# Sample keys turned on VectorE in 32x32 blocks and scored on sixteen 32x32 tiles of TensorE, with the value pages moved to the heads

## The chip, the cores and the metric

The kernel runs on one core of one Trainium2 chip. The metric is device time in microseconds, median of the runs shown. Engines are named as in the profile: PE is TensorE, PEld its weight loads, DVE is VectorE, ACT is ScalarE, POOL is GpSimd, SP issues the DMAs of this kernel.

## The reference

One inference step of a four-layer trunk (short convolution, gated recurrence, differential attention, short convolution) for a prompt of 1024 tokens and a sample group of 8 sequences with 4 new tokens each. The change is in the attention layer's sample group. Its past lies in pages of 128 tokens, found through a page table: 16 pages a sequence, 128 x 1024 float32 (512 KB) each for keys and for values.

```python
def diff_attn_sample(q, k_new, v_new, cache_k, cache_v, page_table, lam):
    bsz, t = q.shape[:2]
    k_past = cache_k[page_table].reshape(bsz, -1, 2 * N_HEADS, HEAD_DIM)
    v_past = cache_v[page_table].reshape(bsz, -1, N_HEADS, V_HEAD_DIM)
    n_past = k_past.shape[1]
    s_past = jnp.einsum('bqhd,bkhd->bhqk', q, k_past).astype(jnp.float32)
    s_new = jnp.einsum('bqhd,bkhd->bhqk', q, k_new).astype(jnp.float32)
    causal = jnp.tril(jnp.ones((t, t), dtype=bool))
    s_new = jnp.where(causal, s_new, -jnp.inf)
    p = jax.nn.softmax(jnp.concatenate([s_past, s_new], axis=-1), axis=-1)
    w = diff_combine(p, lam).astype(v_new.dtype)
    return (jnp.einsum('bhqk,bkhd->bqhd', w[..., :n_past], v_past)
            + jnp.einsum('bhqk,bkhd->bqhd', w[..., n_past:], v_new))
```

There are 16 half heads of 64 features and 8 heads whose values have 128. `diff_combine` subtracts `lam` times the second half head's probabilities from the first's.

## The kernel before, in words

The attention layer has three stages of prompt work. `qkv` makes the q, k and v projections, 512 columns (`n` from 0 to 5) and one 128-token tile (`t`) at a time: 24 matmuls of 128x512 a tile (`qk`, L798), 48 tiles in all. `zpath` makes the gate path (`zz`). `heads` runs prompt attention, head by head and 128 queries at a time: scores `S` (L914), exponentials `P`, transposes `wtp` and the product with the values `pv`.

The sample group is a generator, `sample`, whose steps are mixed into these three by `merge`: each main step adds a share of the sample's estimated cost to a debt, and sample steps run until the debt is paid. The shares are 0.08 and 0.18 in `qkv`, 0.06 in `zpath`, and the rest goes beside the heads. The written order is then arranged by a scheduler, which keeps each engine's dependences.

For each sequence and each pair of pages, `keys` loads two key pages (`kp`, SP, L1083), turns each with eight 128x128 TensorE transposes (`skt`, L1135), copies the result out of PSUM on VectorE and ScalarE in turn (`sk`, L1139), and multiplies the block-diagonal queries `qbd` with it on four column tiles of the array, 128 rows by 32 columns each (`sps`, L1116). `softmax` then makes one exponential over 2080 columns (L1150). `values`, one sequence behind, turns the probabilities (`spt`, L1160), loads value pages (`vp`) and multiplies on four column tiles again (`sacc`, L1175). Pages share four buffers.

A float32 matmul leaves two PE records in the trace: 512 `sps` matmuls of the pages and 64 of the new tokens are 1152 records, 512 `sacc` matmuls 1024.

`page` reads the page number from the table into a register of SP and issues the load from there; a load waits for its buffer to come free, with every later DMA of SP behind it.

Of the kernel before, what the change touches and what calls it, by code (L numbers as in the profile page):

```python
# [35 lines left out]
SAMPLE_COST = NB * (32 * 430 + 8 * 890 + 620 + 4 * 430 + 16 * 400 + 300 + 300.0)  # L36
# [8 lines left out]
class Trunk:  # L45
# [24 lines left out]
    # eight PSUM banks for the whole kernel; each phase deals its kinds of tiles out over the groups of banks  # L70
# [5 lines left out]
    def bank(self, kind, name):  # L76
        tag = next(self.deals[kind])
        return self.psum.tile([128, 512], F32, tag=tag, bufs=self.BANKS[tag], name=name)
# [32 lines left out]
    # keep `inst` behind `first` on their common engine  # L111
# [186 lines left out]
    # features 512 h to 512 h + 511 of one tile, token-major, and their statistics  # L298
# [35 lines left out]
    # the last LayerNorm, with its gain and bias along the rows  # L334
# [34 lines left out]
    # weights of the four products of feature block 0; all at once where the first block goes chunk by chunk  # L369
# [155 lines left out]
    def lru_layer(self, l, u, y, filler):  # L525
# [81 lines left out]
        for s, (kind, i) in enumerate(seq):  # L607
# [4 lines left out]
            elif kind == "xx":  # L612
                # chunks 0 and 1 of both blocks go before chunk 2, which is the last to be there
# [73 lines left out]
    def attn_consts(self, cp):  # L687
# [25 lines left out]
        self.qts = cp.tile([128, KB, S], F32, name="qts")  # L713
        self.kts = cp.tile([128, KB, S], F32, name="kts")
        self.pnew = cp.tile([128, 6, S], F32, name="pnew")
        self.late, self.k_done, self.v_done = [], False, False
# [4 lines left out]
    def qkv(self, u):  # L721
# [42 lines left out]
        def sample_rows(n):  # L764
# [6 lines left out]
            if kind == "q":  # L771
                nc.vector.tensor_scalar(rt[:S], rt[:S], -0.125, None, ALU.mult)
# [745 lines left out]
```

## Time and profile before

| | |
|---|---|
| median of 3 runs | 2516.6 us |
| lowest and highest | 2513.08 and 2520.77 us |
| profiled execution, span from first to last instruction | 2513.0 us (the page gives no other time of this execution) |
| PE, DVE, ACT, POOL busy | 2432.0, 1216.9, 897.1, 195.7 us |
| DMA | 364.14 MB, 145 GB/s on the mean |

The span is the time from the first to the last instruction of one execution on the chip. Busy time is the union of an engine's instructions, so work that overlaps on one engine counts once. A wait is told where the engine sat idle before an instruction, and is put down to what released it.

### The profile page before, as it was taken

What the parts mean: (1) busy time and instruction counts of PE and PEld (TensorE: products, weight loads), DVE (VectorE), ACT (ScalarE), POOL (GpSimd) and SP (SyncE); (2) the same over time, 40 slices, a digit from 0 to 9 for tenths busy, and PEclk for the clock granted to TensorE, in tenths of its full rate; (3) what the DMA queues carried; (4) which work ended last, traced back from release to release, by engine and by line L of the source; (5) the groups of instructions that cost most, each with busy time, mean ns of one, the idle gap of its engine ahead of it and who ended that gap; (6) DMA issues with size and microseconds to landing.
All of it is one profiled execution on the core that took longest, in us unless ns stands there. A gap on an engine that the chain in (4) does not pass through costs nothing.

```text
span 2513.0 us, 41867 instructions
## 1 busy us (share of the span) xinstructions
PE 2432.0 (97%) x16270; PEld 2110.8 (84%) x16270; DVE 1216.9 (48%) x2640; ACT 897.1 (36%) x1837; POOL 195.7 (8%) x329
## 2 busy tenths in 40 slices
PE   7999999999999999999999988989999999999997
PEld 5999999997888897777778966666667999999997
DVE  5323232467466546343323257777775453332355
ACT  4212221246454424122222256667663342222210
POOL 0000000001001000000000023232210000000000
PEclk9999999999999999999999999999999999999999
DMA  9223222433434525254578568888876321111132
GB/s 326 77 84 96 80 77 84 128 96 112 145 123 126 159 66 173 72 161 156 190 268 267 154 192 254 261 253 271 265 268 213 94 73 44 50 43 51 43 117 84
DMA packets 276715, 364.14 MB, mean 145 GB/s; under 512 B 15085, under 2 KB 192622, under 8 KB 276518
## 3 DMA queue, kind: packets, MB, share of 16 engines
q1 hardware_dynamic: 276518, 361.48, 46.3%
q8 instruction: 128, 2.10, 0.4%
q14 instruction: 69, 0.57, 0.1%
HBM read 313.94 MB, written 47.48 MB: 144 GB/s over the span
## 4 chain that ended last, share of the span: by engine, by line
PE 86%; DMA 10%; DVE 1%; ACT 1%; issue 1%; SPq 0%; POOL 0%; DVEq 0%; ACTq 0%; POOLq 0%
PE in L123 30%; PE op L123 15%; PE qk L798 10%; PE xb L123 4%; PE z L123 4%; DMA kp<-cache_k 4%; PE skt L1135 4%; PE zz L123 3%; PE ada L191 2%; PE S L914 2%; DMA tok<-kd 2%; PE sps L1116 2%; PE sacc L1175 2%; PE g L628 2%; PE pv L1009 2%; DMA vp<-cache_v 1%
## 5 line engine op out<-in xcount | busy, mean ns | idle before, releaser
L123 PEld LDWEIGHTS in<-ua,wi 128*128 128x128 f32 x4392 | 707.7, 188 | 22.6 <-issue 14.3
L123 PE MATMUL in<-ua,wi 128*128 128x384 f32 (+1 forms) x4392 | 722.4, 324 | 1.5 <-ACT wi L107 0.8
L798 PE MATMUL qk<-wq,ua 128*128 128x512 f32 x1152 | 288.6, 401 | 0.5 <-ACT qkr L802 0.5
L798 PEld LDWEIGHTS qk<-wq,ua 128*128 128x128 f32 x1152 | 210.6, 188 | 60.7 <-issue 10.8
L1135 PE MATMUL skt<-ident,kp 128*128 128x128 f32 x1024 | 143.2, 275 | 19.5 <-DMA kp<-cache_k 16.1
L1135 PEld LDWEIGHTS skt<-ident,kp 128*128 128x128 f32 x1024 | 115.3, 141 | 47.2 <-issue 12.7
L914 PE MATMUL S<-ks,qhl 128*128 128x512 f32 (+2 forms) x384 | 126.6, 416 | 8.0 <-ACT P L968 6.8
L968 ACT ACTIVATE P<-S,rr 128x512 f32<-128x512 f32 (+2 forms) x192 | 111.0, 584 | 26.7 <-DVE rr L959 14.9
L1139 DVE COPY sk<-skt 128x512 f32<-128x512 f32 x128 | 86.9, 686 | 67.9 <-PE skt L1135 47.8
L955 DVE TENSOR_REDUCE rr<-S 128x1 f32<-128x512 f32 (+2 forms) x192 | 104.2, 550 | 22.7 <-PE S L914 22.2
L283 DVE SCALAR_TENSOR_TENSOR r<-op,gate,xr 128x384 f32<-128x384 f32 (+1 forms) x96 | 54.2, 569 | 118.5 <-PE op L123 81.1
L431 DVE TENSOR_TENSOR sz<-in,sz 128x384 f32<-128x384 f32 (+1 forms) x48 | 25.2, 524 | 176.3 <-PE in L123 176.2
L1139 ACT COPY sk<-skt 128x512 f32<-128x512 f32 x128 | 75.1, 591 | 78.0 <-PE skt L1135 47.2
L123 PEld LDWEIGHTS z<-ub,wrz 128*128 128x128 f32 x576 | 92.6, 188 | 11.7 <-issue 10.1
L123 PE MATMUL zz<-ua,wz 128*128 128x384 f32 (+1 forms) x576 | 102.3, 329 | 0.0
L123 PEld LDWEIGHTS zz<-ua,wz 128*128 128x128 f32 x576 | 92.4, 188 | 7.1 <-issue 7.0
L123 PE MATMUL z<-ub,wrz 128*128 128x384 f32 (+1 forms) x576 | 98.2, 326 | 0.0
L123 PEld LDWEIGHTS xb<-ub,wrx 128*128 128x128 f32 x504 | 81.2, 188 | 12.7 <-issue 9.2
L123 PE MATMUL xb<-ub,wrx 128*128 128x384 f32 (+1 forms) x504 | 88.0, 328 | 0.0
L191 PE MATMUL ada<-wada,ct 128*32 128x512 f32 x384 | 82.9, 624 | 5.2 <-DMA wada<-w_ada 4.1
L1175 PE MATMUL sacc<-vp,pt 128*32 128x256 f32 x1024 | 73.7, 390 | 14.3 <-DMA vp<-cache_v 11.6
L914 PEld LDWEIGHTS S<-ks,qhl 128*128 128x128 f32 x384 | 67.9, 199 | 22.2 <-ACT P L968 10.1
(416 smaller groups left out, 3778.1 us busy)
## 6 DMA issues: line engine op xcount, KB each, us to landing
kp<-cache_k SPq DMA_DIRECT2D x128, 512.0 KB, 4.9
vp<-cache_v SPq DMA_DIRECT2D x128, 512.0 KB, 4.5
wada<-w_ada SPq DMA_DIRECT2D x96, 512.0 KB, 4.7
xa<-xat SPq DMA_DIRECT2D x64, 192.0 KB, 2.8
xr<-xa SPq DMA_DIRECT2D x64, 192.0 KB, 2.6
wi_2r<-a_w_in SPq DMA_DIRECT2D x16, 512.0 KB, 4.1
wi_0r<-a_w_in SPq DMA_DIRECT2D x16, 512.0 KB, 4.5
wi_3r<-a_w_in SPq DMA_DIRECT2D x16, 512.0 KB, 4.2
```

Of the source, the lines that this page charges most:

```text
L123: nc.tensor.matmul(ps[:, :n], wt[:, wp, k], self.ucols(units[k], up, c), start=i == 0, stop=i == 3 * KB - 1)
L191: nc.tensor.matmul(ps[c : c + 32, :], self.ct[:, k], wts[k // 2][:, k % 2], start=k < 4, stop=k >= 4, tile_position=(0, c),)
L283: nc.vector.scalar_tensor_tensor(r[:, :npr], ps[:, :npr], gate[:, d, 0:1], xt[:, :npr], ALU.mult, ALU.add)
L628: nc.tensor.matmul(ps[:, :n], wt[:, wp, q, k, m * 128 : (m + 1) * 128], self.ucols(y[2 * i + k], up, c), start=j == 0, stop=j == 5,)
L798: nc.tensor.matmul(ps, u[k][:, c0 : c0 + 128], wq[n, k // 2][:, wp, k % 2], start=i == 0, stop=i == 3 * KB - 1)
L914: nc.tensor.matmul(st[:, o : o + w], qs[h, g][:, part, s, 128 * qj : 128 * qj + 128], ks[h][:, s, l0 : l0 + w], start=part == 0, stop=part ...
L955: chain(nc.vector.tensor_reduce(rr[:, c : c + 1], t[:, :w], axis=AX.X, op=ALU.min))
L968: nc.scalar.activation(p[:, o : o + w], x["S"][s][i][:, :w], AF.Exp, scale=-1.0, bias=rr[:, 6 + s : 7 + s], accum_out=rr[:, c : c + 1])
L1009: nc.tensor.matmul(x["pv"], x["w"][kb // 4][:, j : j + 128], V[h][:, kb], start=kb == 0, stop=kb == qb)
L1135: nc.tensor.transpose(tp[:, 128 * g : 128 * g + 128], pg[j][:, 128 * h : 128 * h + 128], ident)
L1139: e(kt[:, :, 128 * j : 128 * j + 128], tp.rearrange("p (g t) -> p g t", g=4))
L1175: nc.tensor.matmul(acc[32 * g : 32 * g + 32, :], pts[0][:, 128 * (p % 4) + 32 * g : 128 * (p % 4) + 32 * g + 32], v[:, 256 * g : 256 * g + ...
```

## The change

It rewrites the sample group as two generators. `sample_keys` is mixed into `qkv` (share 0.78 of its cost) and `zpath` (0.24), and whatever is left of it runs out before the heads. `sample_values` is mixed into the heads.

In `sample_keys` a sequence is two halves of 8 pages. Each page is turned by one VectorE instruction, `nc.vector.transpose` on 32x32 blocks, into `kt` (one buffer, 8 pages); page buffers are three. A half is then scored by 128 matmuls of 32 rows, 32 columns and 256 moving columns, one for each of 16 positions of a 4x4 grid of tiles and each `k` of 8, into `psw`, one tile of four PSUM banks with one buffer. One ScalarE copy of 1024 columns takes it out, and the softmax of a sequence follows after its second half, once the new keys are known (`k_done`, set at the first tile of `n` = 3). The probabilities go to DRAM, 1 MB a sequence (`psd`), and `sample_values` reads them back, turns them, and gathers all 16 pages and the new rows in one accumulation. The sample rows of q and k are summed by a matmul with `sel` (`qss`) and turned by VectorE too.

```diff
-SAMPLE_COST = NB * (32 * 430 + 8 * 890 + 620 + 4 * 430 + 16 * 400 + 300 + 300.0)
+KEY_COST = NB * (16 * 300 + 2 * 4000 + 900.0)
+VALUE_COST = NB * (4 * 430 + 16 * 400 + 300 + 300.0)
...
         def sample_rows(n):
             kind, m = "qkv"[n // 2], n % 2
-            ps = acc.pop(n)
-            rt = self.pq.tile([128, 512], F32, tag="rt", bufs=4, name=f"qsr{n}")
-            nc.scalar.copy(rt[:S], ps[0:S])
-            for g in range(1, 4):
-                nc.vector.tensor_tensor(rt[:S], rt[:S], ps[S * g : S * g + S], ALU.add)
-            if kind == "q":
-                nc.vector.tensor_scalar(rt[:S], rt[:S], -0.125, None, ALU.mult)
+            pr = self.pq.tile([128, 512], F32, tag="rt", bufs=3, name=f"qsp{n}")
+            nc.scalar.copy(pr, acc.pop(n))
+            ps = self.tp(f"qss{n}")
+            nc.tensor.matmul(ps, self.sel, pr, start=True, stop=True)
+            rt = self.pq.tile([128, 512], F32, tag="rt", bufs=3, name=f"qsr{n}")
+            nc.scalar.mul(rt, ps, -0.125 if kind == "q" else 1.0)
             if kind == "v":
                 nc.sync.dma_start(
                     a["v_sample"][0, :, :, 4 * m : 4 * m + 4, :].rearrange("b t s f -> (b t) (s f)"), rt[:S]
                 )
                 nc.sync.dma_start(self.vsd[:, 512 * m : 512 * m + 512], rt[:S])
                 return
-            rope(rt, S, 8)
+            rope(rt, 128, 8)
             if kind == "k":
                 nc.sync.dma_start(
                     a["k_sample"][0, :, :, 8 * m : 8 * m + 8, :].rearrange("b t s f -> (b t) (s f)"), rt[:S]
                 )
-            ps = self.tp(f"qst{n}")
-            for j in range(4):
-                nc.tensor.transpose(ps[:, S * j : S * j + S], rt[:S, 128 * j : 128 * j + 128], self.ident[:S, :S])
-            dst = self.kts if kind == "k" else self.qts
-            self.k_done = n == 3
-            nc.vector.tensor_copy(dst[:, 4 * m : 4 * m + 4], ps[:, : 4 * S].rearrange("p (j t) -> p j t", j=4))
+            dst = self.qsb if kind == "q" else self.ksb
+            nc.vector.transpose(dst[:, 16 * m : 16 * m + 16].rearrange("p f t -> p (f t)"), rt)
+            self.q_done, self.k_done = self.q_done or n == 1, n == 3
...
-                if n == 0 and t == 1:
+                if n == 0 and t in (1, 2):
                     for e in range(2):
-                        fetch(0, 2 * e, "s")
-                        fetch(0, 2 * e + 1, "s")
-                        sample_half(0, e)
-                if t == (1 if n == 0 else 0):
+                        fetch(t - 1, 2 * e, "s")
+                        fetch(t - 1, 2 * e + 1, "s")
+                        sample_half(t - 1, e)
+                    sample_rows(t - 1)
+                if n > 1 and t == 0:
                     sample_rows(n)
-                if n < 5 and d in (2, 5):
+                if 0 < n < 5 and d in (2, 5):
                     sample_half(n + 1, d // 3)
                 yield 5120
...
+    def sample_keys(self):
+        nc = self.nc
+        ck, kp = self.pool("smpk", reuse_waits="tile", side="right")
+        self.sp_ = kp
+        self.cpb.__exit__(None, None, None)
+        cw, wp = self.pool("psw", space=PSUM, reuse_waits="tile")
+        self.qsb = kp.tile([128, 32, S], F32, name="qsb")
+        self.ksb = kp.tile([128, 32, S], F32, name="ksb")
+        qb = kp.tile([128, 4, 4, 2, 32], F32, name="qbd")
+        nc.gpsimd.memset(qb, 0.0)
+        half = NPG // 2
+        yield 0
+        while not self.q_done:
+            yield None
+        for b in range(NB):
+            qv = self.qsb.rearrange("p (g x h) t -> p g x h t", x=4, h=2)
+            for x in range(4):
+                nc.gpsimd.tensor_copy(qb[:, :, x, :, 4 * x : 4 * x + 4], qv[:, :, x, :, NQ * b : NQ * b + NQ])
+            qf = qb.rearrange("p g x h c -> p (g x h) c")
+            sc = kp.tile([128, NPG * 128 + S], F32, tag="S", bufs=1, name=f"sc{b}")
+            m = kp.tile([128, 8], F32, tag="smx", bufs=2, name=f"smx{b}")
+            for e in range(2):
+                kt = kp.tile([128, 32, half, 32], F32, tag="kt", bufs=1, name=f"kt{b}_{e}")
+                for j in range(half):
+                    pg = self.page("cache_k", b * NPG + half * e + j, f"kp{b}_{e}_{j}", 3)
+                    nc.vector.transpose(kt[:, :, j], pg.rearrange("p (f t) -> p f t", t=32))
+                    yield 300
+                ps = wp.tile([128, 4, 512], F32, tag="W", bufs=1, name=f"sps{b}_{e}")
+                for k in range(8):
+                    for g in range(4):
+                        for r in range(4):
+                            rows = slice(32 * r, 32 * r + 32)
+                            nc.tensor.matmul(
+                                ps[32 * g : 32 * g + 32, r, : 32 * half], qf[rows, 8 * g + k],
+                                kt[rows, 8 * g + k].rearrange("p j t -> p (j t)"), start=k == 0, stop=k == 7,
+                                tile_position=(32 * r, 32 * g))
+                o = sc[:, 128 * half * e : 128 * half * (e + 1)]
+                nc.scalar.copy(
+                    o.rearrange("p (j r t) -> p r j t", j=half, r=4),
+                    ps[:, :, : 32 * half].rearrange("p r (j t) -> p r j t", j=half))
+                nc.vector.tensor_reduce(m[:, e : e + 1], o, axis=AX.X, op=ALU.min)
+                yield 4000
+            while not self.k_done:
+                yield None
+            ps = self.tps(f"spn{b}")
+            for k in range(8):
                 for g in range(4):
                     nc.tensor.matmul(
+                        ps[32 * g : 32 * g + 32, :S], qf[0:32, 8 * g + k], self.ksb[0:32, 8 * g + k],
+                        start=k == 0, stop=k == 7, tile_position=(0, 32 * g))
+            o = sc[:, NPG * 128 :]
+            nc.vector.tensor_tensor(o, ps[:, :S], self.smask[:, b], ALU.add)
+            nc.vector.tensor_reduce(m[:, 2:3], o, axis=AX.X, op=ALU.min)
+            nc.vector.tensor_reduce(m[:, 3:4], m[:, 0:3], axis=AX.X, op=ALU.min)
+            nc.scalar.activation(sc, sc, AF.Exp, scale=-1.0, bias=m[:, 3:4], accum_out=m[:, 4:5])
+            nc.vector.reciprocal(m[:, 5:6], m[:, 4:5])
+            nc.vector.tensor_tensor(self.coef[:, b : b + 1], m[:, 5:6], self.srow, ALU.mult)
+            nc.sync.dma_start(self.psd[b], sc)
+            yield 900
+        cw.__exit__(None, None, None)
+        ck.__exit__(None, None, None)
+        self.cpb, self.psb = self.pool("psb2", space=PSUM, reuse_waits="tile")
+        self.keys_done = True
...
+    def sample_values(self, y):
+        nc = self.nc
+        ident = self.ident
+        cv, sp_ = self.pool("smpv", reuse_waits="tile", side="right")
+        self.sp_ = sp_
+        vs = sp_.tile([128, D], F32, name="vs")
+        nc.sync.dma_start(vs[:S], self.vsd)
+        def load(b):
+            sc = sp_.tile([128, NPG * 128 + S], F32, tag="S", bufs=2, name=f"sp{b}")
+            nc.sync.dma_start(sc, self.psd[b])
+            return sc
+        nxt = load(0)
+        yield 0
+        for b in range(NB):
+            sc, m = nxt, self.coef[:, b : b + 1]
+            if b + 1 < NB:
+                nxt = load(b + 1)
+            acc = self.tps(f"sacc{b}")[:, :256]
+            def apply(pt, v, k, first):
                 for g in range(4):
                     nc.tensor.matmul(
+                        acc[32 * g : 32 * g + 32, :], pt[:k, 32 * g : 32 * g + 32], v[:k, 256 * g : 256 * g + 256],
+                        start=first, stop=k == S, tile_position=(0, 32 * g))
+            for p0 in range(0, NPG + 4, 4):
+                tp = self.tps(f"spt{b}_{p0}")
+                n = 4 if p0 < NPG else 1
+                w = 128 if p0 < NPG else S
+                for j in range(n):
+                    c = 128 * (p0 + j)
+                    nc.tensor.transpose(tp[:w, 128 * j : 128 * j + 128], sc[:, c : c + w], ident)
+                pt = sp_.tile([128, 512], F32, tag="pt", bufs=2, name=f"pt{b}_{p0}")
+                nc.vector.tensor_copy(pt[:w, : 128 * n], tp[:w, : 128 * n])
+                yield 430
+                if p0 == NPG:
+                    apply(pt, vs, S, False)
+                    continue
+                for j in range(4):
+                    v = self.page("cache_v", b * NPG + p0 + j, f"vp{b}_{p0 + j}", 4)
+                    apply(pt[:, 128 * j : 128 * j + 128], v, 128, p0 + j == 0)
+                    yield 400
+            os_ = sp_.tile([128, 256], F32, tag="os", bufs=2, name=f"os{b}")
+            nc.vector.tensor_scalar(os_, acc, m, None, ALU.mult)
+            self.gather_o(b, os_)
+            yield 300
...
+        cq, self.pq = self.pool("pq", reuse_waits="tile")
+        self.deal(tp="U", tps="U", mm="R")
+        keys = self.sample_keys()
+        next(keys)
+        g = self.qkv(u)
+        for _ in range(3):
+            next(g)
+        merge(g, 45 * 5120.0, keys, self.shares[0] * KEY_COST)
+        cq.__exit__(None, None, None)
+        merge(self.zpath(u), 8 * 10.2 * NT, keys, self.shares[1] * KEY_COST)
+        rest(keys)
...
+        merge(main(), tot, values, VALUE_COST * self.ahead)
+        rest(values)
...
-            self.n_pg, self.n_kt = 4, 2
-            self.shares, self.ahead = (0.08, 0.18, 0.06), 1.2
+            self.shares, self.ahead = (0.78, 0.24), 1.1
```

Three places show what this does to the order of instructions. The first is PE in the projections, before, where the first key pages are turned: rows of `skt` (output, from identity and page `kp`) stand between those of `qk` (projection) and `qkf` (turned projection).

```order
L798 MATMUL qk_0_9759<-wq_3_9581,ua_82 128x512 x3
L1135 MATMUL skt_0_0_0_9854<-ident,kp_0_0_9829 128x128 x4
L1135 MATMUL skt_0_0_1_9860<-ident,kp_0_1_9841 128x128 x4
L1135 MATMUL skt_0_1_0_9867<-ident,kp_0_0_9829 128x128
L811 MATMUL qkf_5_9660<-ident,qkr_5_9652 128x128 x4
L1135 MATMUL skt_0_1_0_9867<-ident,kp_0_0_9829 128x128 x3
L798 MATMUL qk_1_9878<-wq_0_9379,ua_75 128x512 x3
```

PE in the projections, after the change, around the second half of one sequence and the first of the next (`kt_1` and `kt_0`).

```order
L804 MATMUL qk_5_12287<-wq_3_10451,ua_85 128x512 x3
L755 MATMUL qs_12096<-wq_2r,us 32x512 x2
L755 MATMUL qs_12096<-wq_3r,us 32x512 x2
L1129 MATMUL sps_1_11076<-kt_1_10971,qbd 32x256 x128
L1144 MATMUL spn_11725<-ksb,qbd 32x32 x32
L1129 MATMUL sps_0_11358<-kt_0_11253,qbd 32x256 x128
L817 MATMUL qkf_1_11849<-ident,qkr_1_11841 128x128 x4
L804 MATMUL qk_6_12477<-wq_0_10249,ua_78 128x512 x3
```

No `skt` is left; the scores stand in groups of 128, and here two groups follow each other with only the 32 small `spn` matmuls of the new tokens between them.

The second place is VectorE at the same point, with the semaphores that each instruction waits for: `kt` is written from the pages `kp`, one row a page.

```order
L1122 STREAM_TRANSPOSE kt_1_10971<-kp_1_7_11063 128x32x32 [waits DMAHW0_49]
L1122 STREAM_TRANSPOSE kt_0_11253<-kp_0_0_11254 128x32x32 [waits DMAHW1_49,DVE_49,PE_49]
L1122 STREAM_TRANSPOSE kt_0_11253<-kp_0_1_11267 128x32x32 [waits DMAHW2_49]
L1122 STREAM_TRANSPOSE kt_0_11253<-kp_0_2_11280 128x32x32 [waits DMAHW3_49]
L1137 TENSOR_REDUCE smx_10734<-sc_10733 128x1 [waits Activation_49]
L1122 STREAM_TRANSPOSE kt_0_11253<-kp_0_3_11293 128x32x32 [waits DMAHW4_49]
L1150 TENSOR_REDUCE smx_10734<-smx_10734 128x1 [waits DVE_49]
```

The first page of a half waits for PE, that is for the scores of the half before, and each page for its own load; the reductions of the softmax stand between them.

The third place is PE in the heads. Before, 16 transposes of one pair of key pages stand between the prompt's `wtp` and `pv`.

```order
L999 MATMUL wtp_6_512_15882<-ident,P_6_0_15592 128x128 x3
L1235 MATMUL sot_False<-ident,os_14232 128x128 x2
L1135 MATMUL skt_0_0_0_15378<-ident,kp_0_0_15353 128x128 x4
L1135 MATMUL skt_0_0_1_15389<-ident,kp_0_1_15365 128x128 x4
L1135 MATMUL skt_0_1_0_15396<-ident,kp_0_0_15353 128x128 x4
L1135 MATMUL skt_0_1_1_15402<-ident,kp_0_1_15365 128x128 x4
L1009 MATMUL pv_6_15899<-V_14181,wt_6_0_15880 128x128 x4
```

After the change only value work (`sacc`, and `spt`, the turned probabilities read back as `sp`) and the gathering of a finished sequence (`sot`) stand there.

```order
L1006 MATMUL wtp_6_512_16587<-ident,P_6_0_16391 128x128 x3
L1185 MATMUL sacc_15981<-vp_15_16561,pt_12_16464 32x256 x4
L1185 MATMUL sacc_15981<-vs,pt_16_16595 32x256 x4
L1016 MATMUL pv_6_16597<-V_15946,wt_6_0_16585 128x128 x4
L1016 MATMUL pv_6_16597<-V_15946,wt_6_512_16591 128x128 x3
L1230 MATMUL sot_16611<-ident,os_16609 128x128 x2
L1195 MATMUL spt_0_16656<-ident,sp_15979 128x128 x4
```

The key transposes and scores are gone from the heads, and one value page after the other takes four matmuls.

## Rows read from the trace of the kernel before

**Rows 1.** Part 1 of the page, busy us (share of the span) and instructions by engine.

```profile
PE 2432.0 (97%) x16270; PEld 2110.8 (84%) x16270; DVE 1216.9 (48%) x2640; ACT 897.1 (36%) x1837; POOL 195.7 (8%) x329
```

**Rows 2.** Part 4 of the page, the chain that ended last, by engine.

```profile
PE 86%; DMA 10%; DVE 1%; ACT 1%; issue 1%; SPq 0%; POOL 0%; DVEq 0%; ACTq 0%; POOLq 0%
```

**Rows 3.** Tile `qk`: durations min/median/max in ns, first and last start in us.

```profile
L798 PE MATMUL qk<-wq,ua x1152: 387/395/505, 957.5 to 1332.1; 128*128 128x512 f32 x192
```

**Rows 4.** Tile `op`, its third layer.

```profile
L123 PE MATMUL op<-ua,ub1a x288: 288/336/689, 1921.8 to 2012.6; 128*128 128x384 f32 x96, 128*128 128x288 f32 x48
```

**Rows 5.** Windows: length, busy PE PEld DVE ACT POOL, clock, DMA share, GB/s.

```profile
957.00:1458.00 501.00, 496.23 (x3063) 386.67 (x3062) 181.51 (x419) 125.09 (x209) 17.83 (x37) 1.00 0.57 181
1458.00:1922.00 464.00, 419.04 (x3838) 300.36 (x3837) 337.60 (x781) 303.32 (x853) 107.96 (x90) 0.98 0.83 255
```

**Rows 6.** The same windows, tile `skt` alone: busy PE PEld DVE ACT.

```profile
957.00:1458.00 501.00, 51.43 (x378) 43.10 (x379) 31.17 (x47) 27.48 (x47) 1.00 0.57 181
1458.00:1922.00 464.00, 91.77 (x646) 72.18 (x646) 55.74 (x82) 47.62 (x81) 0.98 0.83 255
```

**Rows 7.** The same windows, tile `sps`.

```profile
957.00:1458.00 501.00, 27.78 (x400) 9.59 (x400) 0.36 (x2) 8.63 (x23) 1.00 0.57 181
1458.00:1922.00 464.00, 56.67 (x752) 15.99 (x752) 1.09 (x6) 15.23 (x41) 0.98 0.83 255
```

**Rows 8.** The same windows, tile `vp`: busy PE PEld.

```profile
957.00:1458.00 501.00, 16.51 (x240) 6.67 (x240) 1.00 0.57 181
1458.00:1922.00 464.00, 57.23 (x784) 20.95 (x784) 0.98 0.83 255
```

**Rows 9.** The same windows, tile `spt`: busy PE PEld DVE.

```profile
957.00:1458.00 501.00, 5.06 (x32) 3.92 (x32) 5.51 (x8) 1.00 0.57 181
1458.00:1922.00 464.00, 15.65 (x96) 10.38 (x96) 16.49 (x24) 0.98 0.83 255
```

**Rows 10.** One window, tile `qk`: busy PE PEld ACT.

```profile
1000.00:1075.00 75.00, 68.16 (x279) 50.89 (x278) 6.59 (x11) 1.00 0.32 99
```

**Rows 11.** Groups by line: busy us, mean ns, idle before and releasers.

```profile
L123 PE MATMUL zz<-ua,wz 128*128 128x384 f32 (+1 forms) x576 | 102.3, 329 | 0.0
L108 DVE TENSOR_TENSOR wi<-wi_2r,wi 128x1024 fp32r<-128x1024 f32 x16 | 19.6, 1225 | 62.8 <-ACT wi L107 62.8
L1150 ACT ACTIVATE sc<-sc,smx 128x2080 f32<-128x2080 f32 x8 | 16.3, 2034 | 0.4 <-DVE smx L1149 0.4
```

**Rows 12.** Timeline of PE in the heads: start us, us, instruction, count.

```profile
1701.34 1.07 PE L1175 MATMUL sacc<-vp,pt 128*32 128x256 f32 x16
1704.99 0.63 PE L1135 MATMUL skt<-ident,kp 128*128 128x128 f32 x4 [1.86 <-DMA kp<-cache_k]
1706.57 1.04 PE L1135 MATMUL skt<-ident,kp 128*128 128x128 f32 x8
1707.90 0.64 PE L1116 MATMUL sps<-sk,qbd 128*32 128x256 f32 x8
```

**Rows 13.** Tile `kp`: its DMA issues on SP, and their time to landing.

```profile
L1083 SPq DMA_DIRECT2D kp<-cache_k x128: 337/338/726, 991.9 to 1872.7; - x128
DMA to landing us min/median/max: 3.3/4.9/9.2
```

**Rows 14.** SP's waits, 957 to 1925 us: us in total, times, longest.

```profile
SPq L1083 <- PE sacc L1175: 90.6, 52, 6.5
SPq L1083 <- PE skt L1135: 90.5, 62, 5.3
```

**Rows 15.** Timeline of PE after an idle time of 5.43 us.

```profile
1466.26 0.69 PE L914 MATMUL S<-ks,qhl 128*128 128x384 f32 x1 [5.43 <-ACT P L968]
```

**Rows 16.** Three short windows, columns as in group 5.

```profile
20.00:40.00 20.00, 15.85 (x80) 7.79 (x81) 10.42 (x20) 8.46 (x17) 0.00 (x0) 1.00 1.07 375
1250.00:1275.00 25.00, 23.69 (x166) 17.25 (x165) 10.87 (x16) 7.65 (x12) 0.00 (x0) 1.00 0.98 332
1460.00:1480.00 20.00, 14.02 (x97) 8.72 (x90) 10.89 (x32) 10.84 (x28) 5.87 (x8) 0.74 0.68 194
```

More of the change, by code (lines that the diff above doesn't have):

```diff
@@ L1112, in scores @@
-        def scores(b, kt, n, col, k, mask=None):
-            ps = self.tps(f"sps{b}_{k}")
-            for hl in range(2):
+        cv, sp_ = self.pool("smpv", reuse_waits="tile", side="right")
[7 more added lines that the diff above has]
+        nxt = load(0)
@@ L1190, in sample @@
-        vu = 2
-        for b in range(NB + 1):
-            if b < NB:
-                begin(b)
-            for pp in range(NPG // 2):
-                if b < NB:
-                    yield from keys(b, pp)
-                if b > 0 and (2 * pp + 2) % vu == 0:
-                    yield from values(b - 1, 2 * pp + 2 - vu, vu)
-            if b < NB:
-                while not self.k_done:
-                    yield None
-                softmax(b)
-                yield 620
-            if b > 0:
-                self.gather_o(b - 1, os_[b - 1], False)
-                yield 300
-                if self.v_done:
-                    yield from self.sample_late()
@@ L1274, in attn_layer, with merge @@
     def attn_layer(self, l, u):
         nc = self.nc
-        left = [SAMPLE_COST]
-        smp = self.sample(u)
-        def fill(n):
-            while n > 0 and left[0] is not None:
-                c = next(smp, -1)
-                if c is None:
-                    return n
-                if c < 0:
-                    left[0] = None
-                    return n
-                n -= c
-                left[0] -= c
-            return n
-        def merge(main, total, share):
+        def merge(main, total, side, cost):
@@ L1306, in attn_layer, with rest @@
-        self.v_done = True
-        merge(self.zpath(u), 8 * 10.2 * NT, self.shares[2] * SAMPLE_COST)
-        cq.__exit__(None, None, None)
+                debt += c * cost / total
+                while debt > 0:
+                    n = next(side, -1)
+                    if n is None:
+                        break
+                    if n < 0:
+                        debt = -1e18
+                        break
+                    debt -= n
+        def rest(side):
+            for _ in side:
+                pass
@@ L1311, in attn_layer @@
         tot = 64 * 9 * 110.0 + 288 * 324.0 + 16 * 430
+        values = self.sample_values(u)
+        next(values)
         def main():
```

193 lines of the change are left out of this document (33 added, 160 removed).

## The prediction, made before the changed kernel had run

> **What bounds the kernel now.** I read the page's busy times first, then the chain that ended last, then busy time by stretch, then single tiles. TensorE is busy 97% of the span [rows 1] and carries 86% of the chain [rows 2], so time is saved only by taking work off TensorE, and lost wherever TensorE is made to wait. The attention layer runs from the first `qk` at 957.5 us [rows 3] to the first output projection at 1921.8 us [rows 4], and has two stages. In the projections (957 to 1458) TensorE is busy 496 of 501 us while VectorE has 182 and ScalarE 125; in the heads (1458 to 1922) TensorE has 419 of 464, VectorE 338, ScalarE 303, and the DMA engines are 83% busy at 255 GB/s against 57% and 181 GB/s [rows 5]. So the first stage has VectorE to spare, the second is full on nearly everything.
>
> Most of the sample group's work lies in the second stage: 92 of its 143 us of key transposes [rows 6], 57 of 84 us of scores [rows 7], 57 of 74 us of values [rows 8] and 16 of 21 us of probability transposes [rows 9].
>
> **The change, part by part.** It makes three moves: all keys and scores go to the projections, all values to the heads; keys are turned by VectorE and not by TensorE; scores go through sixteen 32x32 tiles and not four 128x32 ones.
>
> *Stage 1 without sample work.* Two estimates. By busy sums: 501 less 51.4, 27.8, 16.5 and 5.1 [rows 6 to 9] is 400 us. By pace: between 1000 and 1075 us, ahead of any sample work, 279 `qk` matmuls took 75 us with all that goes with them [rows 10], 0.269 us each; 1152 of them [rows 3] make 310, and the gate path's 102 us [rows 11] go on top: 412. Matmuls overlap, so sums of busy time take out too much; I take 412.
>
> *Scores.* One half sequence (8 pages) is 128 matmuls, hence 256 records, because each float32 matmul leaves two (before: 576 matmuls in program order, 1152 records). Sixteen `sacc` records, four tiles side by side, took 1.07 us, eight `sps` records 0.64 [rows 12]: each further round of four costs (1.07 - 0.64)/2 = 0.215 us, and one end about 0.2. The moving operand is 256 columns here as there. With 16 tiles side by side a half needs 16 rounds: 16 x 0.215 + 0.2, about 3.7 us; sixteen halves, 59 us. Bounds: no gain from the row strips (64 rounds) 14 us a half; no round can be shorter, so 3.5 below.
>
> The Trainium skill, "TensorE: Matmul & The Clock Gate", Part 3 (measured speedup), gives 10.6 times for 16 tiles, not 16. By that a half would be 256 x 0.215/10.6, about 5.2 us, and the sum 24 us higher, inside A's range below. No run so far has a row of sixteen tiles.
>
> *Small pieces of stage 1:* eight `spn` groups of 32 small matmuls, six `qss`, about 1 to 2 us each: 15 us (bounds 5 and 30).
>
> *Stalls on VectorE.* The first transpose of a half waits for the last score of the half before (one `kt` buffer), and the first score of a half waits for its eighth page. No row shows a VectorE transpose. The nearest is a 128x1024 float32 tensor_tensor at 1225 ns [rows 11], the same number of elements; I take 1.22 us (bounds 1.1 and 2.45, twice). Three page buffers replace four. A page costs 0.34 us to issue and 4.9 median to land, 3.3 to 9.2 [rows 13]. Three pages wait ready; page 4 comes 0.34 + 4.9 + 1.22 after the first transpose's end, page 7 again that later, page 8 one transpose more: 1.22 + 2 x 6.46 + 1.22 = 15.3 us (12 with 1.1 and 3.3, 24 with 9.2), and some 2 us of VectorE's other work: 17. Cover is what TensorE does between two groups of scores. The sample's softmax waits until the new keys are there (`k_done`), so the third group of scores comes only after 680 of the 1152 `qk` matmuls; from there the gaps hold, by the changed program's order, 40, 0, 48, 57, 38, 65, 66, 53, 57, 52 and 74 projection matmuls, then over 130. At 0.25 us each, 17 less the cover leaves 7 + 17 + 5 + 2.8 + 7.5 + 0.8 + 0.5 + 3.8 + 2.8 + 4 + 0, 51 us; the `spn` and `qss` in those gaps take off about 6: 45 us. With a chain of 12 it is about 15, of 24 about 115. SP adds to this: the store of 1 MB of probabilities waits for the exponential (2.0 us [rows 11]) and the next sequence's page loads are queued behind it; SP already waits 90 us on `skt` and 90 on `sacc` for page buffers [rows 14], so nothing there is free, and I leave it inside the 2 us.
>
> A stall also costs clock: after 5.4 us idle the granted clock over 1460 to 1480 was 0.74 [rows 15, 16], about half of it at 1.2 GHz, some 5 us lost. Two or three of the stalls are that long: 10 us (0 to 20).
>
> Stage 1: 412 + 59 + 15 + 45 + 10 = **541 us, 40 more than now.**
>
> *Heads.* Out go 91.8 of key transposes and 56.7 of scores on TensorE, with 103 us of their copies on VectorE and ScalarE [rows 6]; in come the values and probability transposes of stage 1 (16.5 + 5.1, plus new rows, 25). By busy time 464 - 148.5 + 25 = 340. By slots, since records overlap: eight transposes took 1.04 us and four 0.63 [rows 12], so one more costs 0.10 us; 646 of them are 66 us, 752 score records in rounds of four at 0.215 us 40; in come 60 rounds and 32 transposes, 16 us: 464 - 106 + 16, about 375. By DMA: now 464 us at 255 GB/s, 118 MB, of which 646/1024 of the keys (42 MB) and 784/1024 of the values (51 MB) [rows 6, 8] are the sample's, 25 MB the rest. After: 67 MB of values, 8.5 MB of probabilities read back, 25: 100 MB. At 255 GB/s that is 393 us; at the 332 and 375 GB/s of two short stretches [rows 16], 302 and 268. I take **365, 99 less**, nearest to the slots and a little below, since some of TensorE's 45 idle us here fall on the keys.
>
> Sum: 40 - 99 = -59. On the profiled span of 2513.0 us that is 2454; the median is 3.6 us above that span, so **2458 us.**
>
> **The rivals.**
> *A, as summed: 2458.* Own range 2385 to 2510: the lower end takes 400 for stage 1's own work, 15 for stalls and 340 for the heads (-77), the upper adds most of the bounds of small pieces and stalls (+52).
>
> *B, the tiles pair up badly.* A matmul's two records need the same tile. Where four tiles run, each set of four starts together and the second set a round later [rows 12], which speaks against it. If sixteen were issued as eight, a half would take 7.1 us: +54, 2512, no change. The Trainium skill, same page and part (the mechanism), says that matmuls start and end strictly in program order, which is what would bring this about. By that rule, with both records of a matmul adjacent, the 0.64 us for eight would have been about 1.3, so the trace disagrees for four tiles; for sixteen nothing is shown.
>
> *C, row strips do not run side by side (slower).* Nothing in the trace has two matmuls on different row strips; all tiles there span 128 rows. Then a half is 64 rounds, 14 us: 16 x 10.3 = +165, 2623. It decides at a half of 3.7 + 59/16 = 7.4 us, 33 rounds. Against it: the four column tiles already show two records of one position not blocking others.
>
> *D, VectorE's transposes take twice as long.* 2.45 us a page makes the chain about 23 us and the stalls 110: +65, 2523. For it: no row of the operation, and its output is written in pieces of 32 elements. Against it: the tensor_tensor reads and writes more and takes 1.2.
>
> *E, the heads become DMA-bound.* At today's 255 GB/s 393 us: +28, 2486. For it: TensorE already waits there on pages and the engines are 83% busy. Against it: 332 GB/s over 25 us with the same pages.
>
> **How the numbers follow.** A 0.55, E 0.12, B 0.09, C 0.13, D 0.11. Within 0.3%, some 7.5 us, a measurement cannot tell a change from none. Faster: A, E and 0.02 of B, 0.69. Slower: C, 0.07 of D and 0.03 of B, 0.23. Same: the rest, 0.08. The range runs from A's lower end, 2385, to 2550, past E, B and D, and leaves out C and 0.05 of A: 0.18 in all.
>
> **What would show it.** A half's 256 records: 3.7 us from first to last (A), 7 (B), 14 (C). The transposes' mean: near 1.2 us, not 2.4. The first stage's end, first `S` of the heads: near 1498 us. TensorE's waits for `kt`: some 45 us, the longest right after the first `spn`. The heads near 365 us with the DMA share over 0.9; if that share is 1.0 and TensorE waits on `vp`, it is E. The prediction is wrong if the sixteen tiles take over 7.4 us a half, if the page chain is over 20 us, or if the projections were not as free of other waits as the stretch from 1000 to 1075 us.

## The result and the profile after

The changed kernel takes 2546.6 us (median of 4 runs, 2538.3 to 2555.5), the kernel before 2515.3: a ratio of 1.0129, 95% interval 1.0107 to 1.0152. It is slower by 31 us; the forecast was 2458 and faster. The time lies just inside the top of the stated range; its direction was forecast wrong. Runs of the changed kernel spread over 17 us. The three variants below that have an interval ran four times, the others once, so those are read by their stages and not by a few us of their totals.

The attention layer by stage, cut at the first `S` (columns as in group 5 of the rows above; first stage 1, then the heads):

```profile
957.60:1558.30 600.70, 530.61 (x6626) 408.83 (x6623) 289.35 (x480) 120.47 (x170) 17.03 (x49) 0.95 0.65 215
1558.30:1957.50 399.20, 346.89 (x2707) 232.09 (x2707) 268.58 (x608) 242.74 (x733) 109.72 (x76) 0.94 0.84 245
```

The kernel before, cut in the same way:

```profile
957.50:1452.60 495.10, 491.26 (x3026) 382.11 (x3024) 179.59 (x414) 121.92 (x203) 15.40 (x35) 1.00 0.57 180
1452.60:1921.80 469.20, 423.31 (x3870) 304.27 (x3869) 338.82 (x784) 306.50 (x858) 110.40 (x91) 0.98 0.83 255
```

Stage 1 grew by 106 us, the heads shrank by 70: 36 lost, the whole difference of the spans (2548.0 and 2513.0). TensorE's busy time fell by 37 us over both stages, but its idle time in stage 1 rose from 4 to 70 us; in the heads it is 46 before and 52 after. The groups that answer to [rows 6, 7, 11] (busy, mean ns, idle before and what ended it):

```profile
L1122 DVE STREAM_TRANSPOSE kt<-kp 128x1024 f32<-128x1024 f32 x128 | 155.5, 1233 | 149.7 <-PE sps L1129 90.4 <-DMA kp<-cache_k 58.9
...
L1129 PE MATMUL sps<-kt,qbd 32*32 32x256 f32 x4096 | 100.0, 424 | 44.6 <-DVE kt L1122 24.5 <-issue 20.1
```

VectorE's transpose takes 1233 ns, as forecast. The scores take 100 us, and TensorE waited 24.5 us for `kt` ahead of groups and 20.1 us inside them for nothing that the profile shows ("issue"). Three of the sixteen groups, by window (length, busy PE, PEld and ACT of `sps`, clock, DMA share, GB/s):

```profile
1354.78:1363.24 8.46, 5.53 (x256) 3.70 (x256) 0.00 (x0) 1.00 1.08 359
1378.64:1386.13 7.49, 6.76 (x256) 4.94 (x256) 0.00 (x0) 0.77 0.93 350
1511.07:1516.36 5.29, 5.28 (x256) 3.81 (x256) 0.00 (x0) 1.00 0.26 64
```

The last is undisturbed: 5.28 us. The first has 2.9 us of idle inside, at 359 GB/s; the second follows a wait and runs at a granted clock of 0.77. The same two things in TensorE's timeline, a group with a gap and one without:

```profile
1354.78 3.34 PE L1129 MATMUL sps<-kt,qbd 32*32 32x256 f32 x155
1361.05 2.19 PE L1129 MATMUL sps<-kt,qbd 32*32 32x256 f32 x101 [2.93 <-issue]
...
1511.07 5.28 PE L1129 MATMUL sps<-kt,qbd 32*32 32x256 f32 x256
```

So sixteen groups of 256 records take 120 us, busy and idle inside together, 7.5 each, where 3.7 were forecast.

### The profile page after: what moved, and what is told of

The parts are those of the page before. It is cut to its first block, busy times and chain, and to the rows that moved or that the text cites. A ratio compares the mean times of both kernels' runs of the same rounds, so it can differ in the third digit from the quotient of the medians.

```text
span 2548.0 us, 46254 instructions
## 1 busy us (share of the span) xinstructions
PE 2394.1 (94%) x18696; PEld 2065.3 (81%) x18696; DVE 1252.9 (49%) x2515; ACT 830.0 (33%) x1668; POOL 195.9 (8%) x328
## 4 chain that ended last, share of the span: by engine, by line
PE 81%; DMA 10%; DVE 3%; issue 3%; ACT 1%; SPq 1%; POOL 0%; DVEq 0%; ACTq 0%; POOLq 0%
PE in L126 29%; PE op L126 14%; PE qk L804 8%; PE xb L126 4%; PE z L126 4%; PE sps L1129 4%; DMA vp<-cache_v 3%; DMA kp<-cache_k 3%; PE zz L126 3%; PE ada L194 2%; PE sacc L1185 2%; PE S L921 2%; PE pv L1016 2%; PE g L631 2%; DVE kt L1122 1%
## 5 line engine op out<-in xcount | busy, mean ns | idle before, releaser
L804 PEld LDWEIGHTS qk<-wq,ua 128*128 128x128 f32 x1152 | 217.6, 192 | 67.6 <-ACT qkr L808 10.2
L1122 DVE STREAM_TRANSPOSE kt<-kp 128x1024 f32<-128x1024 f32 x128 | 155.5, 1233 | 149.7 <-PE sps L1129 90.4
L1129 PE MATMUL sps<-kt,qbd 32*32 32x256 f32 x4096 | 100.0, 424 | 44.6 <-DVE kt L1122 24.5
L1129 PEld LDWEIGHTS sps<-kt,qbd 32*32 32x32 f32 x4096 | 67.2, 108 | 73.6 <-issue 54.6
L1185 PE MATMUL sacc<-vp,pt 128*32 128x256 f32 x1024 | 87.9, 405 | 29.0 <-DMA vp<-cache_v 25.5
L126 PE MATMUL zz<-ua,wz 128*128 128x384 f32 (+1 forms) x576 | 94.6, 324 | 0.0
L1016 PEld LDWEIGHTS pv<-V,wt 128*128 128x128 f32 x576 | 75.3, 199 | 23.7 <-ACT wt L1008 13.3
L1016 PE MATMUL pv<-V,wt 128*128 128x128 f32 x576 | 85.3, 291 | 6.1 <-ACT wt L1008 6.1
```

Of the source, the lines that this page charges most:

```text
L126: nc.tensor.matmul(ps[:, :n], wt[:, wp, k], self.ucols(units[k], up, c), start=i == 0, stop=i == 3 * KB - 1)
L804: nc.tensor.matmul(ps, u[k][:, c0 : c0 + 128], wq[n, k // 2][:, wp, k % 2], start=i == 0, stop=i == 3 * KB - 1)
L1016: nc.tensor.matmul(x["pv"], x["w"][kb // 4][:, j : j + 128], V[h][:, kb], start=kb == 0, stop=kb == qb)
L1122: nc.vector.transpose(kt[:, :, j], pg.rearrange("p (f t) -> p f t", t=32))
L1129: nc.tensor.matmul(ps[32 * g : 32 * g + 32, r, : 32 * half], qf[rows, 8 * g + k], kt[rows, 8 * g + k].rearrange("p j t -> p (j t)"), start ...
L1185: nc.tensor.matmul(acc[32 * g : 32 * g + 32, :], pt[:k, 32 * g : 32 * g + 32], v[:k, 256 * g : 256 * g + 256], start=first, stop=k == S, t ...
```

## The experiments

A gap is idle time of TensorE inside a group of scores. Theory I: the groups of scores are slow through their number of instructions, and their cost is on the path; the heads are TensorE's busy time plus an idle time that stays. Rivals: the tiles do not run side by side (columns), VectorE's chain is the loss, the heads are limited by the DMA engines.

**Half and a quarter of the columns**, with the same number of matmuls (the second with `half // 4` and `8 * half`).

```diff
-                                ps[32 * g : 32 * g + 32, r, : 32 * half], qf[rows, 8 * g + k],
-                                kt[rows, 8 * g + k].rearrange("p j t -> p (j t)"), start=k == 0, stop=k == 7,
+                                ps[32 * g : 32 * g + 32, r, : 16 * half], qf[rows, 8 * g + k],
+                                kt[rows, 8 * g + k, : half // 2].rearrange("p j t -> p (j t)"), start=k == 0, stop=k == 7,
...
```

The part left out of the diff copies the scores that exist to the places of those that do not.

> Each score matmul moves 128 columns and not 256, so the scores of half the pages are left out; the number of matmuls stays. If a group of scores is paced by the rate at which TensorE's instructions come (16.7 ns a record in the middle of a group of the changed kernel, 256 records), an undisturbed group stays at 4.4 to 5.3 us (5.3 before this edit) and the sixteen together stay above 95 us (121); total 2520 to 2550. If it is paced by the tiles, that is by columns, an undisturbed group falls to about 2.7 us, the sixteen to 65 us or less, total 2490 or less.

> Each score matmul moves 64 columns, so the scores of three quarters of the pages are left out; the number of matmuls stays. The undisturbed groups of 256 and 128 columns took 5.28 and 3.69 us: a fixed 2.10 us (8 ns a record) and 12.4 ns a record for each 256 columns. By that an undisturbed group takes 2.9 us here, and the sixteen still more than 75 us with their gaps. If the fixed part is the spacing of 14 to 17 ns seen inside the groups, it stays at 3.4 us or more.

Measured: 2535.0 and 2525.2 us. An early group in the changed kernel, with 128 and with 64 columns, the first two without a gap, the last with one of 0.35 us:

```profile
1183.57:1188.86 5.29, 5.28 (x256) 3.81 (x256) 0.00 (x0) 1.00 0.62 245
```

```profile
1184.84:1188.54 3.70, 3.68 (x256) 3.28 (x256) 0.00 (x0) 1.00 0.52 208
```

```profile
1187.30:1190.65 3.35, 3.00 (x256) 2.60 (x256) 0.00 (x0) 1.00 0.47 188
```

Neither pure reading holds: 5.28, 3.68 and 3.00 us busy is close to a fixed 2.1 us and 3.2 us for 256 columns, which is sixteen rounds of 0.2 us (another group of 128 columns took 4.07 from its first record to its last). The column part is what the forecast had; the fixed part it lacked. What the fixed part hangs on is not shown. 256 records at 8 ns fit it, and so do sixteen rounds at 0.13 us, which is near the time of one weight load; each record has its own:

```profile
L1129 PEld LDWEIGHTS sps<-kt,qbd x4096: 101/104/173, 1027.7 to 1515.8; 32*32 32x32 f32 x196
```

(Durations min/median/max in ns.) No run changed the number of records or of weight loads and kept the columns. And the idle time inside the groups grows as the tiles get less to do:

```profile
L1129 PE MATMUL sps<-kt,qbd 32*32 32x128 f32 x4096 | 68.5, 298 | 33.0 <-issue 32.4 <-DVE smx L1151 0.5
```

```profile
L1129 PE MATMUL sps<-kt,qbd 32*32 32x64 f32 x4096 | 51.2, 236 | 39.0 <-issue 39.0
```

Busy and idle inside: 120, 101 and 90 us for 256, 128 and 64 columns. Most of the 120 us stays when three quarters of the columns go, so most of it does not hang on the columns. The totals fall by less than the groups do: in both runs the granted clock of stage 1 is 0.92 and not 0.95, and `qk` is busy for 298 and 300 us, not 287.

**The inner loops exchanged.**

```diff
-                    for g in range(4):
-                        for r in range(4):
+                    for r in range(4):
+                        for g in range(4):
```

> The two inner loops of the score matmuls change places: consecutive matmuls now differ in column and not in row strip; nothing is left out. If a fixed cost for each instruction and the columns set the pace of a group, an undisturbed group stays at 5.28 us (within 0.2) and the total at 2540 to 2556. If neighbouring row strips of one column hinder each other, an undisturbed group changes by 0.5 us or more, sixteen of them by 8 us or more.

2542.8 us; an undisturbed group is 5.28 us again. These two orders of the tiles make no difference.

**No loads of key pages** but the first three.

```diff
-                    pg = self.page("cache_k", b * NPG + half * e + j, f"kp{b}_{e}_{j}", 3)
+                    if len(pgs) < 3:
+                        pgs.append(self.page("cache_k", b * NPG + half * e + j, f"kp{b}_{e}_{j}", 3))
+                    pg = pgs[j % len(pgs)]
...
```

> Only the first three key pages are loaded, and all transposes read these; the key loads of the other pages are left out. If the gaps inside the groups (21 us in all) are instruction supply that page loads delay, they fall below 8 us, a group is 5.3 to 5.8 us, the chain of transposes falls from 15 to 10 us, waits for it (24 us) to near nothing and the granted clock in the groups to 1.00: the sixteen groups take about 88 us, not 121, total about 2490. If the gaps are TensorE's own, they stay near 20 us and the total is about 2510.

2534.4 us, far from 2490. The gaps did shrink and so did the waits for `kt`:

```profile
L1132 PE MATMUL sps<-kt,qbd 32*32 32x256 f32 x4096 | 98.6, 408 | 18.2 <-DVE kt L1125 10.5 <-issue 7.6
```

So page loads lengthen the gaps (20.1 us with them, 7.6 without), but of the 26 us won here stage 1 kept 10: the groups' busy time stays, and TensorE now waits 13.4 us on `qkr` ahead of `qk`, where it waited 3.6.

What the gaps are, the trace can say. Among the DMA queues on the page (packets, MB, share of 16 engines' span) is one of instructions, before and after:

```profile
q8 instruction: 128, 2.10, 0.4%
q8 instruction: 147, 2.41, 0.4%
```

TensorE's records, PE and PEld, are 32540 and 37392: 254 to a packet in both kernels, so q8 brings TensorE its instructions, 16 KB at a time. In the changed kernel each of the 14 gaps over 0.25 us (19.9 us in sum) ends 1.2 to 1.6 us after one of these packets has ended, whether the gap is 0.4 or 3.1 us long. So do the 9 gaps of this run (7.6 us), the 15 with 64 columns (39.0 us) and the only one with early rows and divided groups (2.9 us). Some 47 packets came in the 490 us that hold all the groups, so this is not chance: TensorE sits in the gaps until its next instructions have come. Why there is less of this without page loads stays open: the packets themselves take 1.0 us at the median in both runs.

**One k step of eight**, 7/8 of the score matmuls left out.

```diff
-                for k in range(8):
+                for k in range(1):
...
```

> Only the first of the eight k steps of each group of scores is computed, seven eighths of the score matmuls are left out; transposes, loads, copies and softmax stay. If the sixteen groups cost what they span, 121 us less 8, and stalls stay as they are, the total is about 2435 to 2455. If they only fill time in which TensorE would wait for the chain of transposes, the waits grow and it is 2480 or more.

2452.1 us, 95 less; stage 1 is 508 us, the wait for `kt` 24.0. The scores are on the path with nearly all that they span, and the waits for the chain do not grow into the room.

**Early rows of k**, so that `k_done` comes with the fifth token tile.

```diff
-                if n == 0 and t in (1, 2):
+                if n == 0 and t in (1, 2, 3, 4):
...
-                if n > 1 and t == 0:
+                if n > 3 and t == 0:
...
-                if 0 < n < 5 and d in (2, 5):
+                if 2 < n < 5 and d in (2, 5):
```

> The sample rows of k are projected right after those of q, at the third and fourth token tile, so that the softmax of a sequence need not wait for the column block n = 3 and the sixteen groups of scores spread over all of the projections; 4 MB of weights are loaded twice more. If the waits for the transposes (24 us) and the lower clock in the groups (15 us) come from crowding after that wait, both go: 2505 to 2520. If they come back as other waits (projection copies, page loads), 2535 or more.

2537.7 us, ratio to before 1.0090, interval 1.0070 to 1.0109. The waits for `kt` fall from 24.5 to 3.3 us, the gaps to 11.5, most groups run at a clock of 1.00, and stage 1 is 582 us, 19 less. The gain that was expected (28 us or more) did not come: the groups still take 101 us busy, and other idle time, over 30 us in many pieces (weights of the early rows, `qkf`, `qss`), remains.

**Divided groups**: eight pieces of 16 matmuls, each kept behind the projection matmul written last; `qkv` yields after every three matmuls, and the shares in `merge` follow. Alone, and with early rows.

```diff
...
                                 tile_position=(32 * r, 32 * g))
+                            if g == 0 and r == 0:
+                                self.after(mi, self.last_mm)
+                    yield 1
...
```

> Each group of 128 score matmuls is put in eight pieces of 16 matmuls (32 records) with at least three projection matmuls between them where the written order allows it; the new keys still come late, so about half of the groups stay whole. If a long group is slow because TensorE's instructions come too slowly (the first 32 records of a group start 7 ns apart, the rest 17 ns), the divided groups cost 3.6 to 5 us and not 7.5, and the total is 2510 to 2535. If the tiles themselves set the pace, nothing is gained and the changes of tiling add to it: 2545 to 2570.

> Early rows of k and divided groups together; nothing is left out. By instruction supply: 128 pieces of 0.45 to 0.55 us each, 64 us, no gaps inside, no stall on the transposes, clock near 1.00: stage 1 at 500 to 515 us, total 2455 to 2475. If the tiles run only 10.6 times side by side, 128 pieces of 0.66 us and a total near 2490. If each change between tilings costs some 0.3 us, 2510 or more.

2561.0 and 2568.5 us (the second 1.0214 of before, 1.0194 to 1.0235): the gain that instruction supply was to bring did not come; the branches that charge changes of tiling gave the totals. TensorE's timeline with both:

```profile
1180.78 0.96 PE L804 MATMUL qk<-wq,ua 128*128 128x512 f32 x3
1181.67 0.71 PE L1132 MATMUL sps<-kt,qbd 32*32 32x256 f32 x32
1182.32 0.95 PE L804 MATMUL qk<-wq,ua 128*128 128x512 f32 x3
1183.20 0.71 PE L1132 MATMUL sps<-kt,qbd 32*32 32x256 f32 x32
```

A piece and three projections repeat every 1.53 us (1183.20 - 1181.67). Three projections alone are 3 x 68.16/279 = 0.73 [rows 10], so a piece costs 0.8 us where an eighth of an undisturbed group costs 0.66. With both edits the gaps are nearly gone (2.9 us in all; 15.7 with the division alone), and the groups' own busy time is nearly that of early rows alone, 102.3 us against 100.9. Yet stage 1 is 617 us against 582. TensorE's busy time is 19 us more, and 112 pieces more at 0.14 us would be 16; its idle time is 15 us more, with a new wait of 26.7 us (5.1 with early rows alone):

```profile
PE qkf L819 <- DVE qkr L770: 26.7, 11, 6.5
```

So the changes of tiling are, by this estimate, about half of what was lost, and waits of `qkf` (us, times, longest) for VectorE, in an order that has changed, outweigh the gaps that went. The Trainium skill, "TensorEngine Tiling (Array Packing)", Key Properties, says that a change of tiling mode drains TensorE. The trace agrees as far as it goes: a piece of 32 records between projections costs 0.14 us more than an eighth of a group that changes once. How much of that is a drain no run separates.

**Values without loads, later values, few values.** Four value pages loaded and reused; `self.ahead` 0.95 in place of 1.1; and one value page of sixteen loaded and multiplied.

```diff
-                    v = self.page("cache_v", b * NPG + p0 + j, f"vp{b}_{p0 + j}", 4)
+                    if len(pgs) < 4:
+                        pgs.append(self.page("cache_v", b * NPG + p0 + j, f"vp{b}_{p0 + j}", 4))
+                    v = pgs[j]
```

```diff
-                    v = self.page("cache_v", b * NPG + p0 + j, f"vp{b}_{p0 + j}", 4)
-                    apply(pt[:, 128 * j : 128 * j + 128], v, 128, p0 + j == 0)
+                    if p0 + j == 0:
+                        v = self.page("cache_v", b * NPG + p0 + j, f"vp{b}_{p0 + j}", 4)
+                        apply(pt[:, 128 * j : 128 * j + 128], v, 128, p0 + j == 0)
```

> Only the first four value pages are loaded and then used for all; the other loads of value pages are left out. If the heads are paced by the DMA engines while values come in (1558 to 1898 us, share about 1.0, 270 to 320 GB/s), the heads fall from 400 to 345 us or less, total about 2490. If TensorE and ScalarE set the pace there, the heads stay above 385 us, total 2535 or more.

> The sample's values are spread over the heads at 0.95 of their cost and not 1.1; nothing is left out. If the heads are paced by the DMA engines until the values end 60 us before the heads do, spreading them saves 8 to 25 us: total 2522 to 2540. If not, the total stays within 5 us of 2548, or is longer by what is left to the end.

> Fifteen of sixteen value pages of each sequence are neither loaded nor multiplied; probability transposes stay. If the heads are TensorE's busy time plus some 50 us of waits that stay (347 + 52 in the changed kernel), they fall by what the value products occupy there, some 45 to 60 us, to 340 to 355 and the total to about 2490 to 2505. If the prompt's own chain (scores, maximum, exponential, transposes, product) sets the pace and the values only fill its gaps, the heads stay at 385 us or more and the total at 2530 or more.

2544.0, 2547.2 and 2502.2 us. Spreading the values changed nothing that a single run can show. Without loads, and without the value products, the heads are:

```profile
1558.00:1952.60 394.60, 342.64 (x2709) 241.07 (x2707) 269.40 (x608) 243.76 (x732) 106.79 (x76) 0.97 0.29 82
```

```profile
1561.80:1909.80 348.00, 275.60 (x1747) 214.26 (x1746) 265.54 (x607) 240.38 (x732) 109.12 (x76) 0.93 0.36 99
```

At 82 GB/s and 29% the heads are 5 us shorter: the DMA engines, 84% busy in the changed kernel, do not set the pace. TensorE then waits for the exponentials where it waited for pages. Without the products the heads fall by 51 us, TensorE's busy time by 71, and idle time rises to 72. So busy time that leaves the heads comes back in part only, 51 of 71 us here, and no removal took the idle time away.

**The placement alone**: after's generators, with the loops of the kernel before for transposes and scores.

```diff
-                    nc.vector.transpose(kt[:, :, j], pg.rearrange("p (f t) -> p f t", t=32))
+                        tp = wp.tile([128, 512], F32, tag="W", bufs=4, name=f"skt{b}_{pp}_{hl}_{j}")
+                        for g in range(4):
+                            h = 2 * g + hl
+                            nc.tensor.transpose(tp[:, 128 * g : 128 * g + 128], pg[j][:, 128 * h : 128 * h + 128], ident)
...
```

> The placement alone: keys in the projections, values in the heads, probabilities through DRAM, as in the changed kernel, but keys turned by TensorE and scored on four column tiles as in the kernel before; nothing is left out. If the placement is the loss (the heads give back less than the projections take), stage 1 is near 587 us and the heads 400: total 2525 to 2550. If the loss is in VectorE's turning and the sixteen tiles, the total is 2500 to 2518, the kernel before or better.

2577.0 us, 1.0243 of before (1.0213 to 1.0273): slower than both theories had it. By stage:

```profile
956.30:1588.40 632.10, 620.23 (x4147) 454.51 (x4145) 233.12 (x525) 200.97 (x345) 20.57 (x60) 0.99 0.61 199
1588.40:1984.70 396.30, 343.90 (x2756) 231.10 (x2754) 269.31 (x611) 241.90 (x733) 107.11 (x75) 0.96 0.85 256
```

This splits the change in two. Putting all keys beside the projections and all values beside the heads, with the probabilities through DRAM and the new sample rows that go with it, costs 64 us in these two stages (58 by the medians): the heads give back 73, stage 1 takes 137. TensorE's busy time rises by 129 us in stage 1 and falls by 79 in the heads. Turning on VectorE and scoring on sixteen tiles, which no run takes apart, then give back 30: stage 1 is 31 us shorter than here, with 90 us less of TensorE's busy time and 58 us more of idle time. No version that computes everything beats the kernel before. VectorE's turning with the placement of before was not tried: it would need the four PSUM banks of the scores, and 32 KB a partition for `kt`, during the heads.

## Why the prediction was wrong, by its own steps

- *Scores, 59 us: the step that failed most.* Measured 120 (100.0 busy, 20.1 idle inside). The columns cost what sixteen tiles side by side should (3.2 us a half), and 16 records of an undisturbed group start in its first 0.11 us, so A's mechanism, and neither B's 7.1 us nor C's 14. The step that failed is that a round costs only its columns: an undisturbed group has a fixed 2.1 us more, and the term had nothing for late instructions either. "No round can be shorter" was right. The change made 4096 score records of 1152, and no row of before was a dense stream of that kind. The Trainium skill, "TensorE: Matmul & The Clock Gate", Part 3, has 10.6 times for sixteen tiles; the estimate that the prediction made from it, 5.2 us a half, agrees with the undisturbed 5.28. The other 2.2 us of the mean are the gaps (1.3) and 1.0 more of busy time, most of it in the six groups with a granted clock of 0.67 to 0.82.
- *Heads, 365 us: the second step that failed.* Measured 399. Both sums in the text (340 by busy time, 375 by slots) kept the 45 idle us and took out busy time of TensorE, 123 and 90 us net; the term went ten below the slots. Busy time fell by 76 (423.3 to 346.9), and 52 us stayed idle. That the 340 is near the measured busy time of 347 is chance: it stood for busy and idle together. One part of the shortfall shows on the pages, the same 1024 records of value products before and after (busy us, mean ns, idle before):

```profile
L1175 PE MATMUL sacc<-vp,pt 128*32 128x256 f32 x1024 | 73.7, 390 | 14.3 <-DMA vp<-cache_v 11.6
L1185 PE MATMUL sacc<-vp,pt 128*32 128x256 f32 x1024 | 87.9, 405 | 29.0 <-DMA vp<-cache_v 25.5
```

  They are busy 14 us longer. The rest, records that overlapped others and so left little room, and a granted clock of 0.94 where it was 0.98, no run takes apart. By E's number (393) the heads look limited by the DMA engines; the run without loads shows that they are not.
- *Stage 1 without scores: right in its sum, in part by luck.* 412 + 15 + 45 + 10 = 482 was forecast; 600.7 - 120.1 = 481 was measured. The parts moved: waits for `kt` 24.5 and not 45, in return 25 us of other waits (`qss`, `qs`, `spn` among them) that the sum did not have.
- *VectorE's transposes: right.* 1233 ns against 1.22 us; the chain of eight pages against 15.3 us is 15.1 in this group, first start to last end (1338.50 to 1353.58; the rows of `kt` in VectorE's timeline, whose other work lies between them):

```profile
1338.50 3.50 DVE L1122 STREAM_TRANSPOSE kt<-kp 128x1024 f32<-128x1024 f32 x3 [7.54 <-PE sps L1129]
1343.57 1.25 DVE L1122 STREAM_TRANSPOSE kt<-kp 128x1024 f32<-128x1024 f32 x1 [0.48 <-DMA kp<-cache_k]
1346.22 1.25 DVE L1122 STREAM_TRANSPOSE kt<-kp 128x1024 f32<-128x1024 f32 x1 [1.32 <-DMA kp<-cache_k]
1347.53 1.25 DVE L1122 STREAM_TRANSPOSE kt<-kp 128x1024 f32<-128x1024 f32 x1
1350.08 1.25 DVE L1122 STREAM_TRANSPOSE kt<-kp 128x1024 f32<-128x1024 f32 x1 [0.20 <-DMA kp<-cache_k]
1352.35 1.23 DVE L1122 STREAM_TRANSPOSE kt<-kp 128x1024 f32<-128x1024 f32 x1
```

  Three pages, then waits for the buffers' next loads: D did not come about.
- *The sum.* -59 + 61 (scores) + 34 (heads) = +36; the spans differ by 35. The break-even stood in the text: 7.4 us a half. The mean is 7.5, and the heads did the rest. In A's own range the three values named for the lower end give -67; -77 needs the 10 us of clock as well.

That the gaps inside the groups are TensorE's instructions arriving late is shown by the ends of the q8 packets. What makes up the fixed 2.1 us of a group without gaps stays open: of theory I the cost on the path and the late instructions are shown, a cost of each instruction is not.

## What to carry to other kernels

Cost a dense stream of small matmuls by more than its columns: here a group of 256 records had 2.1 us beside the 3.2 us of its columns, and waited for its instructions on top of that. When work is taken off the bounding engine in a stage, do not take its summed busy time out of the stage: here 76 us went where 123 were summed, and the idle time stayed. Two moves in one change are priced apart: here the engines earned 30 us and the placement lost about 60.

## What the runs showed of the hardware that was not expected

- TensorE's instructions come by DMA, 254 records to a packet of 16 KB. In groups of some 512 records without other work between them TensorE can run out of them: it then stood still for 0.4 to 3.1 us, 20 us in all, each time until 1.2 to 1.6 us after a packet had ended. Shorter matmuls made this 39 us.
- A group of 256 records on sixteen tiles took 5.28 us busy with 256 columns, 3.68 with 128 and 3.00 with 64; at 256 columns both orders of the tiles took 5.28.
- The same TensorE transposes and scores cost more beside projections than beside the heads: with all of them there, stage 1 took 137 us more than before, and the heads gave back 73.
- TensorE's idle time in the heads lay between 46 and 72 us with 423 to 276 us of work in them, and with 82 to 255 GB/s beside it.
